# Moving the modulation tiles, the tap tables and the long convolution within a two-layer trunk

## The chip, the cores and the metric

The kernel runs on one core of a Trainium2 chip. The metric is the device time of one execution in microseconds: the median of three runs is 1769.27 us (1768.16 to 1769.97). The core has a matrix engine (PE; PEld is its weight load, which overlaps the products), a vector engine (DVE), a scalar engine (ACT), a second vector-like engine (POOL) and SP, which here issues DMAs. Each takes its instructions in the order in which they stand in its queue, and waits for the others by semaphores.

## The reference

Two layers over 640 tokens (128 context tokens and 512 latent ones) with 1024 channels. Each layer is a mixer and a feed-forward part; each of the two is preceded by a norm, which is scaled and shifted by a modulation that comes from a conditioning vector, and added to the stream through a gate from the same modulation:

```python
mod = silu(cond) @ w_mod[i] + b_mod[i]               # 6 x 1024 values, for 2 kinds of tokens
sh1, sc1, gt1, sh2, sc2, gt2 = split(mod, 6)
hm  = rmsnorm(x, g_mix) * (1 + sc1) + sh1
x   = x + gt1 * mixer(hm)
hf  = rmsnorm(x, g_ffn) * (1 + sc2) + sh2
x   = x + gt2 * conv_ffn(hf)

# mixer of layer 0
proj = hm @ w_in                                     # z, xbc, dt, and the two halves of glu
xbc  = silu(conv5(xbc)); y = ssd_scan(both ways); y_ssd = rmsnorm(y * silu(z))
u    = glu[:1024] * sigmoid(glu[1024:])
u    = silu(layernorm(conv31(u)))                    # the long convolution, per channel
out  = concat(y_ssd, u) @ w_out
```

The mixer of layer 1 is a Fourier transform over tokens and channel groups, with a linear map behind it.

## The kernel before

A channel tile is 128 channels on the partitions and the tokens along the free dimension; 1024 channels are eight tiles. Each product of an fp32 weight tile with the activations is done as three products of split numbers (high by high, high by low, low by high), 48 matmuls of 128x320 per output tile (`mtile`, L233). The weights are split on ACT (a cast) and on POOL (a subtraction). A product collects in a bank pair of PSUM (`acc`); small results use half banks (`misc`).

The order of the work in layer 0 is the order of the code, except where `tc.issue_after(x)` sets the priority of what it holds behind the instruction x. The stages, with their place in the span:

- The start (0 to 74 us). x is loaded, its squares are summed on ACT and DVE (`SumSq`, L330 and L334), and the norm's factor is made (L306). Then for each channel tile k the shift column is made by `mod_tensor` and the scale column by `mod_vector`, the tile is normed and split (`norm_split`), and three products (time steps, first half of the first gated pair) take one tile after another as it comes.
- The gated pairs (74 to 222 us), the loop at L839. Each of eight rounds has two products (14 in all, since the first pair is begun at the start); ACT makes a tanh, DVE the gated product `ut` (L851). Behind each gating come four modulation tiles (`MODSG`), and in the last four rounds some steps of the long convolution (`CONV`).
- The projection of group 0 (222 to 265 us), four products, each followed by a convolution of width 5 on DVE and by one step of the long convolution (`CONVP`).
- The scan (265 to about 500 us): four groups of five chunks. Chunk i+1 is begun (`scan_a`: decay exponents and weights), the fillers of chunk i follow (`project` of the next group, the gates' products, and five steps of the long convolution by `CONVAT`), then `scan_b` (chunk product) and `scan_c` (sum into y, next state). It is written one chunk ahead, so that PE has something between dependent pieces.
- The output products (about 500 to 699 us), first those of y, then those of u, each tile ending in a residual on DVE (L366); between the residuals stand 16 modulation tiles (`YMODS`, `UMODS`).
- The feed-forward part of layer 0 (to 1130 us), with 32 more modulation tiles; the Fourier mixer (to 1297 us); the feed-forward part of layer 1 (to 1769 us). Each works on pairs of channel tiles: two products of about 7 us, a 3x3 convolution on DVE, POOL and PE, and a gating.

Modulation. Of the 96 columns, the first 8 shifts are made on PE (`mod_tensor`, L248: eight matmuls of a weight tile with the 2 conditioning vectors as stationary operand, a copy of the 2 rows, a transpose to columns). All others are made row by row on DVE (`mod_vector`, L272): SP fetches a 128x1024 tile of the transposed weights, and two instructions (L280) multiply it with a conditioning row that has been broadcast to all partitions, and sum along the row; L284 adds the bias. The broadcast rows (`cond_rows`, L266) are fetched from memory by a broadcasting DMA and put through Silu, three times: for the start, for the gated pairs, and for the output products.

The long convolution (`conv_steps`, L590) works in the frequency domain on blocks of 98 tokens. It is a generator of 16 steps; a step has up to three parts on different blocks: `turn` (transposes on PE, copy on ACT), `forth` (transform on PE, two products with the tap tables on DVE), `back` (transform back on PE, addition on DVE, sums on POOL). The tap tables (`tap_tables`, L561) are four small matmuls of the taps with a transform matrix and four copies on ACT, behind DMAs on ACT's queue. They stand ahead of the gated loop (L838).

What the names in the rows mean: `con` the identity and masks, `vec` the small vectors, `crow` the broadcast rows, `mraw` and `rawv` a modulation weight tile, `modc` the finished columns, `mjunk`/`junk` the unused product, `tt` and `tw` the transform matrix and the taps, `dfl` the transform of the long convolution, `cv` its middle, `u` its input and output, `yT` the stream, `yh`/`uh` the split y and u, `wh` the high weights, `xh` the normed activations.

## Time and profile before

| | |
|---|---|
| median of three runs | 1769.27 us |
| profiled execution | 1770.86 us, its span 1769.1 us |
| instructions | 27926 |
| DMA | 194.98 MB, mean 110 GB/s |
| PE's granted clock, mean | 0.969 |

The profile is one execution. Its page gives busy times of each engine over the span; a busy PE is a PE whose matmuls follow one another, at whatever clock was granted. The windows view gives the same for chosen stretches, with the granted clock (1.00 is the upper of its two levels, 2.4 GHz). The timeline gives instructions in order of time with the idle time before them and what ended it. The groups by line add up instructions of one line and form. In every view `128x320 f32` is partitions by elements, and `x12` a count.

### The profile page before, as it was taken

The page shows a single profiled execution, that of the slowest core. Times are in us where ns is not written, and L with a number is a line of the kernel's source. Part 1 is how long each engine was busy: PE and PEld are TensorE (multiplying, and loading weights), DVE is VectorE, ACT ScalarE, POOL GpSimd, SP SyncE. Part 2 cuts the span into 40 slices and gives each one's busy share as a digit, 9 for nine tenths or more (in the row PEclk, how much of TensorE's full clock was granted, in tenths as well). Part 3 has the DMA queues.
Part 4 walks back from the last instruction along what each step waited for, and adds up shares of the span by engine and source line. Part 5 has one row for each costly group of instructions (what it writes and reads, how often), then busy time and mean ns, then how long its engine had stood idle before and what let it go on. Part 6 is the DMA issues. An engine that isn't in the chain of part 4 may idle for free.

```text
span 1769.1 us, 27926 instructions
## 1 busy us (share of the span) xinstructions
PE 1640.6 (93%) x10769; PEld 1574.7 (89%) x10769; DVE 1350.1 (76%) x2392; ACT 700.4 (40%) x1221; POOL 833.0 (47%) x566
## 2 busy tenths in 40 slices
PE   5789999999989878999999999989799999999996
PEld 3589998888968867999999999969799999999996
DVE  6778776677379887899889999873878738817846
ACT  4323154687656134332232133355543313312324
POOL 1134235555667443555455365512536535544544
PEclk8889999999989988999999999989999999999998
DMA  7545431333224543215323522431522222222123
GB/s 284 198 157 192 144 99 60 99 99 112 84 83 155 191 144 120 87 54 152 117 64 115 184 66 62 132 104 42 175 82 69 69 84 79 65 84 72 57 58 113
DMA packets 84677, 194.98 MB, mean 110 GB/s; under 512 B 7843, under 2 KB 35394, under 8 KB 84544
## 3 DMA queue, kind: packets, MB, share of 16 engines
q1 hardware_dynamic: 81216, 189.43, 34.2%
q10 hardware_dynamic: 3328, 3.77, 0.7%
q8 instruction: 85, 1.39, 0.3%
q14 instruction: 48, 0.39, 0.1%
HBM read 189.33 MB, written 3.83 MB: 109 GB/s over the span
## 4 chain that ended last, share of the span: by engine, by line
PE 56%; DVE 10%; ACT 2%; issue 1%; DMA 1%; POOL 1%; DVEq 0%; SPq 0%; ACTq 0%; POOLq 0%
PE acc L233 53%; DVE mm L280 2%; DVE yT L366 2%; DVE ssq L334 2%; DVE hmt L352 1%; PE acc L341 1%; PE misc L233 1%; PE acc L1100 1%; DVE xl L361 1%; ACT sqt L330 1%; DVE yT L1240 1%; DVE modc L284 0%; PE acc L1208 0%; DVE ul L945 0%; DMA mm<-in_condr 0%
## 5 line engine op out<-in xcount | busy, mean ns | idle before, releaser
L225 POOL TENSOR_TENSOR wl<-raw,wh 128x512 fp32r<-128x512 f32 (+5 forms) x324 | 577.8, 1791 | 748.6 <-ACT wh L222 741.4
L233 PE MATMUL acc<-xh,wh 128*128 128x320 f32 (+2 forms) x2064 | 489.6, 315 | 14.9 <-ACT xh L360 6.8
L1038 DVE SCALAR_TENSOR_TENSOR cva<-acc,cw,cva 128x504 f32<-128x504 f32 (+2 forms) x704 | 482.8, 693 | 18.5
L222 ACT CAST wh<-raw 128x512 fp32r<-128x512 f32 (+5 forms) x324 | 244.1, 764 | 628.9 <-PE acc L233 488.9
L233 PE MATMUL acc<-xh,wl 128*128 128x320 f32 (+2 forms) x2064 | 490.6, 314 | 0.0
L233 PE MATMUL acc<-xl,wh 128*128 128x320 f32 (+2 forms) x2064 | 488.8, 314 | 0.4 <-DVE xl L361 0.4
L233 PEld LDWEIGHTS acc<-xh,wh 128*128 128x128 f32 (+1 forms) x2064 | 353.7, 191 | 18.0 <-issue 8.9
L233 PEld LDWEIGHTS acc<-xh,wl 128*128 128x128 f32 (+1 forms) x2064 | 352.7, 190 | 3.6 <-issue 2.5
L233 PEld LDWEIGHTS acc<-xl,wh 128*128 128x128 f32 (+1 forms) x2064 | 352.7, 191 | 3.0 <-DVE xl L361 1.5
L233 PE MATMUL acc<-fh,wl 128*128 128x320 f32 (+2 forms) x832 | 206.1, 310 | 2.8 <-POOL wl L225 2.7
L233 PE MATMUL acc<-fh,wh 128*128 128x320 f32 (+2 forms) x832 | 206.1, 310 | 0.0
L233 PE MATMUL acc<-fl,wh 128*128 128x320 f32 (+2 forms) x832 | 205.7, 310 | 0.0
L366 DVE SCALAR_TENSOR_TENSOR yT<-acc,modc,yT 128x512 f32<-128x512 f32 (+4 forms) x233 | 108.1, 492 | 113.4 <-PE acc L233 111.3
L233 PEld LDWEIGHTS acc<-fh,wl 128*128 128x128 f32 x832 | 143.2, 188 | 4.5 <-POOL wl L225 4.2
L233 PEld LDWEIGHTS acc<-fl,wh 128*128 128x128 f32 x832 | 143.4, 188 | 0.6
L233 PEld LDWEIGHTS acc<-fh,wh 128*128 128x128 f32 x832 | 143.3, 188 | 0.4
L280 DVE SCALAR_TENSOR_TENSOR mm<-mm 128x1024 f32<-128x1024 f32 x84 | 129.3, 1540 | 3.5 <-DMA mm<-in_w_modT 2.7
L1027 DVE SCALAR_TENSOR_TENSOR cva<-acc,cw,cva 128x127 f32<-128x127 f32 x176 | 61.3, 348 | 69.8 <-ACT cva L1023 64.4
L280 DVE SCALAR_TENSOR_TENSOR mjunk<-mraw,crow 128x1024 f32<-128x1024 f32 x64 | 88.5, 1383 | 4.6 <-DMA mraw<-in_w_modT 4.1
L1070 POOL TENSOR_TENSOR fl<-cva,fh 128x640 fp32r<-128x640 f32 x44 | 70.4, 1600 | 35.2 <-ACT fh L1069 35.2
L1066 POOL TENSOR_TENSOR cva<-cva 128x640 f32<-128x640 f32 x44 | 69.8, 1586 | 17.1 <-ACT cva L1065 17.1
L1069 ACT CAST fh<-cva 128x640 fp32r<-128x640 f32 x44 | 32.0, 728 | 100.8 <-POOL cva L1066 100.8
(252 smaller groups left out, 1941.6 us busy)
## 6 DMA issues: line engine op xcount, KB each, us to landing
raw<-in_ffn_w_up SPq DMA_DIRECT2D x88, 512.0 KB, 3.6
mm<-in_w_modT SPq DMA_DIRECT2D x42, 512.0 KB, 3.7
raw<-in_w_in SPq DMA_DIRECT2D x40, 512.0 KB, 3.7
mraw<-in_w_modT SPq DMA_DIRECT2D x32, 512.0 KB, 3.8
e<-acsd SPq DMA_DIRECT2D x40, 256.0 KB, 3.5
raw<-in_ffn_w_down SPq DMA_DIRECT2D x32, 256.0 KB, 2.7
mraw<-in_w_mod SPq DMA_DIRECT2D x14, 512.0 KB, 4.1
raw<-in_ffn_w_down SPq DMA_DIRECT2D x16, 448.0 KB, 3.4
```

Of the source, the lines that this page charges most:

```text
L222: S.copy(wh[:, ks, :], raw[:, ks, :])
L225: G.tensor_tensor(wl[:, ks, :], raw[:, ks, :], wh[:, ks, :].bitcast(F32), op=SUB)
L233: PE.matmul(part(ps, s), lhsT=wt[:, k, :], rhs=tok(at, s), start=(k == 0 and p == 0), stop=(k == n - 1 and p == 2))
L280: V.scalar_tensor_tensor(junk, in0=raw[:, cs_], scalar=1.0, in1=crow[j][:, cs_], op0=MULT, op1=MULT, accum_out=m[:, 2 * o + j:2 * o + j + 1])
L330: S.activation(t, tok(x_ap, s), AF.Square)
L334: V.tensor_tensor(tok(self.a, s), tok(self.a, s), t, op=ADD)
L366: last = V.scalar_tensor_tensor(tok(x[:, m, :], sub), in0=part(ps, s, o, sub), scalar=gt[:, m, j:j + 1], in1=tok(x[:, m, :], sub), op0=MUL ...
L1027: V.scalar_tensor_tensor(a[:, lo:hi], in0=ps[:, BASE + lo + d:BASE + hi + d], scalar=w(1, c), in1=a[:, lo:hi], op0=MULT, op1=ADD)
L1038: last = V.scalar_tensor_tensor(av[:, r0:r1, c0:c1], in0=pv[:, r0 + dr_:r1 + dr_, c0 + dc:c1 + dc], scalar=w(r, c), in1=av[:, r0:r1, c0:c1 ...
L1066: G.tensor_tensor(cv[0], cv[0], cv[1], op=MULT)
L1069: S.copy(h_, cv[0])
L1070: G.tensor_tensor(l_, cv[0], h_.bitcast(F32), op=SUB)
```

## The change

The broadcast rows are made once, at the start: ACT fetches the two conditioning rows as a 2x1024 tile (`crow2`), puts it through Silu, and PE spreads each row to 128 partitions by a product with a selecting matrix (`sel`, made on DVE from the identity); DVE copies them to SBUF, where they stay until the scan ends. The three fetches of broadcast rows go. The tap tables are made at the start too: their four DMAs stand on ACT's queue ahead of the Silu of the rows and the squares, the four matmuls and two copies behind the norm's sums. For the channel tiles 0, 3 and 6 the scale column is made on PE, together with the shift (`SCPE`). The gated rounds have 2, 3, 4, 4, 4, 3, 3, 3 modulation tiles (26 in place of 32). The scan gets 16, one behind the weights of each of its first 16 chunks (`MODSC`). The output products have none. Six go to the first six pairs of the last feed-forward part (`MODS1`). The modulation weight tiles outside the start have two buffers in place of three (`MRAW`). The nine steps of the long convolution that are left after the gated pairs are done within the projection of group 0 (3, 2, 2, 2) in place of one behind each of its four products and one in each of the first five turns of the scan; its buffers are closed before those of the scan are opened, ahead of the fourth product's convolution.

```diff
-SCPE = ()
-MODSG = (4,) * 8
+SCPE = (0, 3, 6)
+MODSG = (2, 3, 4, 4, 4, 3, 3, 3)
+MODSC = (1,) * 16 + (0,) * 4
-CONVP = 1
-CONVAT = {0: 1, 1: 1, 2: 1, 3: 1, 4: 1}
+CONVP = (3, 2, 2, 2)
-YMODS = (0,)*5+(2,2,1,1,0,0,0,0)
-UMODS = (2,2,2,2,2,0,0,0)
-MRAW = 3
+MRAW = 2
-MODS1 = ({}, ((0,) * 8,) * 3)
+MODS1 = ({j: 1 for j in range(6)}, ((0,) * 8,) * 3)
...
+    con = one.tile([P, 3 * P], F32, name="con")
+    S.dma_start(con, A["consts"])
     vec = one.tile([P, NV], F32, name="vec")
     S.dma_start(vec, A["vec"])
-    con = one.tile([P, 3 * P], F32, name="con")
-    S.dma_start(con, A["consts"])
...
+        crow2 = sp.tile([P, D], F32, name="crow2")[0:2, :]
+        S.dma_start(crow2, A["condr"])
+        tw = [temp(f"tw{h}")[0:CK, 0:HC] for h in range(2)]
+        tt = sp.tile([P, 2 * P], F32, name="tt")[0:CK, :]
+        S.dma_start(tt, A["dftk"])
+        for h in range(2):
+            S.dma_start(tw[h], A["conf_w"][:, HC * h:HC * h + HC])
+        S.dma_start(dfl, A["dftl"])
         for k in range(0, KD, 2):
             nc.sync.dma_start(xin[:, k:k + 2, 0:T], A["xT"][:, k:k + 2, :])
-        crow = cond_rows(sp)
+        S.activation(crow2, crow2, AF.Silu)
+        sel = sm.tile([P, 384], F32, tag="sqt", name="sel", bufs=3)[0:2, 0:2 * P]
+        prow = []
+        for j in range(2):
+            V.tensor_copy(sel[:, P * j:P * j + P], ident[0:2, j:j + 1].broadcast_to([2, P]))
+            prow.append(acc())
+            for h in range(2):
+                PE.matmul(prow[j][:, HC * h:HC * h + HC], lhsT=sel[:, P * j:P * j + P], rhs=crow2[:, HC * h:HC * h + HC], start=True, stop=True)
         rsqrt_table(eps)
...
+        for j in range(2):
+            V.tensor_copy(crow[j], prow[j])
...
-        for t in crow:
-            S.activation(t, t, AF.Silu)
+        for i in range(2):
+            ps = acc()
+            for h in range(2):
+                PE.matmul(ps[:, HC * h:HC * h + HC], lhsT=tt[:, P * i:P * i + P], rhs=tw[h], start=True, stop=True)
+            S.copy(tap[i], ps)
...
-            V.scalar_tensor_tensor(e1[:, h, :], in0=cm[:, 0, :], scalar=dt[:, c, i:i + 1], in1=e1[:, h, :], op0=MULT, op1=ADD)
+            last = V.scalar_tensor_tensor(e1[:, h, :], in0=cm[:, 0, :], scalar=dt[:, c, i:i + 1], in1=e1[:, h, :], op0=MULT, op1=ADD)
+        with tc.issue_after(last.ins):
+            mods_n(MODSC[5 * g + c])
...
-    mcrow = cond_rows(md)
-    for t in mcrow:
-        S.activation(t, t, AF.Silu)
-    mjunk = md.tile([P, D], F32, name="mjunk")
...
-    tap_tables()
...
-    md_.__exit__(None, None, None)
+    first = project(0, R[0])
+    for f, n in zip(first[:3], CONVP):
+        f()
+        convolve(n)
+    convolve(CONVP[3])
+    assert next(conv, 0) == 0
+    cw_.__exit__(None, None, None)
+    cp_.__exit__(None, None, None)
     mz = tc.tile_pool(name="mz", bufs=1)
     mzp = mz.__enter__()
-    for f in project(0, R[0]):
-        f()
-        convolve(CONVP)
+    first[3]()
...
-    for i, n in CONVAT.items():
-        fillers[i].append(lambda n=n: convolve(n))
...
     def after_w(m, ps):
-        with tc.issue_after(residual(x, m, ps, gt, ALL).ins):
-            mods_y(UMODS[m])
+        residual(x, m, ps, gt, ALL)
```

How this stands in the queues of the engines, at three places. First ACT's queue from its beginning. A number behind a name tells tiles of one name apart; `DMAHW0` to `DMAHW7` are eight landing counters that the DMAs use in turn. Before:

```order
L172 DMA cond_75<-in_cond 128x16
L174 DMA vec_77<-in_vec 128x280
L176 DMA con_79<-in_consts 128x384
L300 ACT_TABLE_LOAD
L300 ACTIVATE tab_112<-eps_84 128x1 [waits DVE_49]
L244 ACT_TABLE_LOAD
L244 ACTIVATE sc__86<-cond_75 128x16 [waits DMAHW0_49]
L330 ACTIVATE ssq_115<-xin_94 128x320 [waits DMAHW1_49]
```

And with the change:

```order
L172 DMA con_77<-in_consts 128x384
L174 DMA vec_79<-in_vec 128x280
L438 DMA crow2_117<-in_condr 2x1024
...
L441 DMA tt_121<-in_dftk 31x256
L443 DMA tw0_119<-in_conf_w 31x512
L443 DMA tw1_120<-in_conf_w 31x512 [waits DMAHW2_49]
L444 DMA dfl_111<-in_dftl 128x324 [waits DMAHW3_49]
L447 ACTIVATE crow2_117<-crow2_117 2x1024 [waits DMAHW4_49]
L290 ACT_TABLE_LOAD
L290 ACTIVATE tab_140<-eps_83 128x1 [waits DVE_49]
L320 ACTIVATE ssq_142<-xin_93 128x320 [waits DMAHW1_49]
```

The first square (L330, now L320) has moved behind the issue of the tap tables' DMAs, two of which wait for the landing of con and vec, and behind the Silu of the short rows.

Second DVE's queue in the scan, in one chunk of group 0 (`w` the weights, `e` the exponents, `hn` the next state, `cm` the chunk's masked product, `y` and `yT` sums). Before:

```order
L787 SCALAR_TENSOR_TENSOR w<-cm,dt,w 128x128 x4
L803 TENSOR_TENSOR e<-misc,eacs 128x512
L770 TENSOR_TENSOR e<-e 128x512
L728 TENSOR_TENSOR hn<-misc,hd 128x256
L822 TENSOR_TENSOR yT<-misc,yT 128x128 x2
L777 TENSOR_TENSOR cm<-misc,con 128x256
L813 TENSOR_TENSOR y<-misc,y 128x256
```

And with the change:

```order
L802 SCALAR_TENSOR_TENSOR w<-cm,dt,w 128x128 x3
L270 SCALAR_TENSOR_TENSOR mjunk,mm<-mraw,crow_106 128x1024
L839 TENSOR_TENSOR yT<-misc,yT 128x128
L270 SCALAR_TENSOR_TENSOR mjunk,mm<-mraw,crow_107 128x1024
L839 TENSOR_TENSOR yT<-misc,yT 128x128
L274 TENSOR_SCALAR modc_87<-mm,vec 128x2
L785 TENSOR_TENSOR e<-e 128x512
L743 TENSOR_TENSOR hn<-misc,hd 128x256
L830 TENSOR_TENSOR y<-misc,y 128x256
```

Two products of a modulation tile and its bias now stand between the chunk's weights and the exponents, the next state and the sum of y that follow.

Third DVE's queue in the output products of u (L366 and L356 are the residuals). Before:

```order
L366 SCALAR_TENSOR_TENSOR yT<-acc,modc_88,yT 128x512
L280 SCALAR_TENSOR_TENSOR mm_5230,mm<-mm_5230 128x1024
L366 SCALAR_TENSOR_TENSOR yT<-acc,modc_88,yT 128x128
L284 TENSOR_SCALAR modc_89<-mm,vec 128x2
L280 SCALAR_TENSOR_TENSOR mm_5230,mm<-mm_5230 128x1024
L366 SCALAR_TENSOR_TENSOR yT<-acc,modc_88,yT 128x512
```

And with the change:

```order
L356 SCALAR_TENSOR_TENSOR yT<-acc,modc_87,yT 128x128
L356 SCALAR_TENSOR_TENSOR yT<-acc,modc_87,yT 128x512
L356 SCALAR_TENSOR_TENSOR yT<-acc,modc_87,yT 128x128
L356 SCALAR_TENSOR_TENSOR yT<-acc,modc_87,yT 128x512
```

Between the residuals nothing of the modulation is left.

## Rows read from the trace of the kernel before

**Rows 1.** The profile's page: busy time of each engine, share of the span, instructions.

```profile
PE 1640.6 (93%) x10769; PEld 1574.7 (89%) x10769; DVE 1350.1 (76%) x2392; ACT 700.4 (40%) x1221; POOL 833.0 (47%) x566
```

**Rows 2.** Windows: stretch, us, PE, PEld, DVE, ACT, POOL busy, PEclk, DMA share, GB/s.

```profile
1350.00:1375.00 25.00, 25.00 (x172) 25.00 (x171) 22.96 (x39) 9.03 (x12) 15.88 (x8) 1.00 0.19 52
```

**Rows 3.** Windows of the projection, the scan's first three groups, the output products.

```profile
222.00:265.00 43.00, 42.50 (x289) 39.24 (x287) 32.80 (x51) 26.38 (x52) 16.57 (x17) 1.00 0.31 95
265.00:332.00 67.00, 61.66 (x398) 56.31 (x398) 43.04 (x82) 32.89 (x70) 38.37 (x48) 0.97 0.25 76
332.00:385.20 53.20, 50.14 (x340) 48.02 (x340) 37.79 (x79) 40.94 (x88) 28.61 (x33) 1.00 0.35 99
385.20:435.80 50.60, 45.98 (x301) 42.34 (x300) 38.75 (x82) 41.30 (x93) 28.88 (x32) 1.00 0.36 104
550.00:650.00 100.00, 82.15 (x540) 79.65 (x538) 91.26 (x141) 35.99 (x58) 61.87 (x38) 0.94 0.53 173
```

**Rows 4.** Timeline: start us, us, engine, line, operation [idle before <- releaser], the start.

```profile
5.27 0.81 ACT L330 ACTIVATE ssq<-xin 128x320 f32<-128x320 f32 x2
...
7.93 0.19 DVE L180 TENSOR_SCALAR vec<-vec 128x56 f32<-128x56 f32 x1 [6.10 <-DMA vec<-in_vec]
...
12.95 1.99 ACT L439 ACTIVATE crow<-crow 128x1024 f32<-128x1024 f32 x2
...
14.96 1.28 ACT L306 ACT_TABLE_LOAD   x1
...
30.97 0.74 PE L233 MATMUL acc<-xh,wh 128*32 128x320 f32 x2 [4.23 <-ACT xh L360]
```

**Rows 5.** DMA issues of the first 30 us: KB each, median us to landing.

```profile
con<-in_consts ACTq DMA_DIRECT2D x1, 192.0 KB, 8.3
```

**Rows 6.** Groups by line, PE, 31 to 73.9: busy us, mean ns, idle before.

```profile
L254 PE MATMUL misc<-mraw,sc__86 128*2 128x128 f32 x80 | 9.9, 272 | 0.0
```

**Rows 7.** Timeline of PE around its longest waits before the scan.

```profile
83.77 3.75 PE L569 MATMUL misc<-tw,tt 31*128 31x512 f32 x4 [9.88 <-DMA tt<-in_dftk]
...
90.96 1.98 PE L569 MATMUL misc<-tw,tt 31*128 31x512 f32 x4
...
122.65 0.88 PE L233 MATMUL acc<-xh,wh 128*128 128x320 f32 x2 [5.66 <-DVE u L851]
```

**Rows 8.** Windows right behind the first and the last of these waits.

```profile
87.45:92.87 5.42, 5.42 (x18) 3.84 (x17) 2.38 (x5) 2.68 (x4) 0.00 (x0) 0.68 0.02 6
122.65:128.65 6.00, 6.00 (x23) 6.00 (x24) 6.00 (x17) 0.00 (x0) 0.00 (x0) 0.51 0.38 117
```

**Rows 9.** Groups by line, DVE, gated pairs from 87 to 222 us.

```profile
L280 DVE SCALAR_TENSOR_TENSOR mjunk<-mraw,crow 128x1024 f32<-128x1024 f32 x53 | 74.8, 1411 | 0.9 <-DMA mraw<-in_w_modT 0.6
...
L284 DVE TENSOR_SCALAR modc<-mm,vec 128x2 f32<-128x2 f32 x26 | 11.7, 452 | 0.3
...
L280 DVE DVE_READ_ACCUMULATOR mjunk<-mraw,crow 128x1 f32 x52 | 4.2, 81 | 0.0
```

**Rows 10.** Line L280 in the same stretch: shortest, median, longest in ns.

```profile
L280 DVE SCALAR_TENSOR_TENSOR mjunk<-mraw,crow x53: 1208/1223/2311, 87.1 to 221.9; 128x1024 f32<-128x1024 f32 x53
```

**Rows 11.** Windows of tile dfl (PE, PEld), long convolution in the scan.

```profile
265.00:340.00 75.00, 13.60 (x88) 10.87 (x88) 0.98 0.25 78
```

**Rows 12.** The same of tile u (PE, PEld, DVE, ACT, POOL).

```profile
265.00:340.00 75.00, 1.80 (x12) 1.42 (x12) 2.67 (x5) 0.00 (x0) 5.79 (x6) 0.98 0.25 78
```

**Rows 13.** The same of tile cv (PE, PEld, DVE).

```profile
265.00:340.00 75.00, 9.89 (x80) 9.63 (x80) 5.48 (x8) 0.98 0.25 78
```

**Rows 14.** Waits of the whole span: total us, times, longest.

```profile
PE acc L233 <- DVE yT L366: 8.0, 6, 2.5
```

**Rows 15.** Timeline of PE in the output products.

```profile
546.27 0.38 PE L233 MATMUL acc<-yh,wh 128*128 128x256 f32 x1 [1.87 <-ACT yh L896]
...
588.39 0.55 PE L233 MATMUL misc<-yh,wh 128*128 128x256 f32 x1 [6.43 <-DVE yT L366]
...
595.09 0.53 PE L233 MATMUL acc<-uh,wh 128*128 128x320 f32 x2 [1.67 <-issue]
```

More of the change, by code (lines that the diff above doesn't have):

```diff
@@ L434, in _body @@
                 ss.add(xin[:, k, :], k, s)
+        for j in range(2):
+            V.tensor_copy(crow[j], prow[j])
+        V.tensor_scalar_mul(vec[:, 0:NGAIN], vec[:, 0:NGAIN], -0.5 / D)
         bc0 = ss.bc
@@ L471, in _body @@
         pd, pg0, pa0 = (ps for ps, _ in first)
[L473 to L474 removed]
+    cw_ = tc.tile_pool(name="cw", bufs=1)
+    cw = cw_.__enter__()
     def t640(name):
@@ L597, in forth @@
             PE.matmul(ps, lhsT=dfl[:, 0:P], rhs=xt.pop((h, b)), start=True, stop=True)
-            vv[h, b] = [mxp.tile([P, HC], F32, tag=f"cv{i}", name=f"cv{i}", bufs=2) for i in range(2)]
+            vv[h, b] = [cw.tile([P, HC], F32, tag=f"cv{i}", name=f"cv{i}", bufs=2) for i in range(2)]
             for i in range(2):
@@ L972, in _body @@
                 y_segment(CHUNKED[c == 4])
-    assert next(conv, 0) == 0
     mz.__exit__(None, None, None)
+    md_.__exit__(None, None, None)
     mx.__exit__(None, None, None)
@@ L978, in _body @@
     yp = yp_.__enter__()
[L979 to L986 removed]
     def after_w(m, ps):
[L990 to L991 removed]
+        residual(x, m, ps, gt, ALL)
     while ytodo:
         n = ny - len(ytodo)
[L995 to L996 removed]
+        y_product()
         if n == LNY:
```

92 lines of the change are left out of this document (36 added, 56 removed).

## The prediction

> **What bounds the kernel now.** I read the page first, then the busy times by stage, the timeline of PE around its longest waits, the groups of instructions by line, and the waits. On the page the reader is to see that PE is busy for 93% of the span [rows 1], so only what keeps PE waiting, or what it does besides the products, can give time back. By stage this is not spread evenly. The two feed-forward parts hold PE at 25 of 25 us [rows 2]; nothing is to be had there. PE waits in three other places: around the end of the first norm and the tap tables (0 to 129 us), in the scan (265 to 436 us, where PE is busy 61.7 of 67.0, 50.1 of 53.2 and 46.0 of 50.6 us [rows 3]), and in the output products after it (550 to 650 us, where DVE is busy 91.3 of 100 and PE 82.2 [rows 3]). The change touches all three. All sums are made against the profiled execution, 1770.86 us (span 1769.1 and 1.8 around it); it lies 1.6 above the median of the runs, and I take that off at the end.
>
> **The start, up to the first gated product: +2 us.** Two things are moved here, the tap tables and the broadcast of the conditioning rows, and three scale tiles go from DVE to PE. Before, ACT started its squares at 5.27 us [rows 4]. In the new order ACT first issues four more DMAs, and two of them wait for the landing of con and vec, because DMAs share eight landing counters in turn. The con DMA, issued third before, took 8.3 us to land [rows 5], until about 10.0 us of the span; vec was there at 7.93 [rows 4]. With their order swapped I take 10.0 for the later one. Behind it stand the Silu of the short rows (free length 1024, half of the 1.99 us of two such [rows 4]) and a table load of 1.28 [rows 4]: squares at about 12.3 us, 7 later. A table load and two tap copies of 1024 (1.0 each by the same row) stand among them, another 3. The first main product would be released about 10 us later than 30.97 [rows 4], but before it waited for DVE, whose two row-wise tiles stood between the norm and hmt; I take 8. PE then also has 3 more tiles of the small product, 1.98 us each (9.9 us for five tiles [rows 6]): 6 us, of which 4.9 tiles of all now stand ahead of the first main product, beside the late norm. From there to the end of the stretch (73.9 us, where the wait of 9.88 begins [rows 7], 42.9 us after the first product) DVE has five row-wise tiles less, 15 us at their shortest price of 3.0 (below). PE's own need is 144 products at 0.145 (172 in 25 us [rows 2]), 6.1 tiles of 1.98, and about 3 of transposes: 36 instead of 42.9. So +8 - 6 = +2. From both sides: -6 if vec and con land as early as 8 us and the rest hides, +10 if the main stretch stays as long as it is.
>
> **The stretch of gated products: -23.8 us.** Behind the last product of the start PE stands for 9.88 us until the tap tables' data lands, and then spends 3.75 on two of the four tap products [rows 7]: the next product comes at 87.45, 13.55 us late. The following 5.42 us run at a granted clock of 0.68 [rows 8], between the two levels of 1.2 and 2.4 GHz, after PE had stood; a third of it, 1.7, is lost. The other two tap products take 1.98 [rows 7]. All of that goes, if the tables are made while PE has nothing to do at the start. Then there is one wait of 5.66 for DVE's gating [rows 7], followed by 6.00 us at 0.51 of the clock [rows 8], 2.9 lost: DVE came to that gating late because four row-wise tiles stood ahead of it, held by rows that were still landing and being put through Silu, and the time-step arithmetic as well. With two and three tiles in the first two rounds instead of four and four it is in time. Sum 25.8. I give back 2: the buffers for the row-wise tiles are cut from three to two, so the rows of a tile can be asked for only when the tile before the last is done. The bounds are -28, and -15 if DVE stays late.
>
> What is late next is DVE in each round. A row-wise tile costs two L280 of 1.41, two reads of the accumulator (0.08) and one L284 of 0.45 [rows 9, 10]: 3.43 us, and at the least 2 x 1.21 + 0.16 + 0.45 = 3.0. Four are 13.7 of a round of 14 (96 products), so DVE nearly fills it; with three of them in rounds 5 to 7 it is looser than before.
>
> **The scan: +23.6 us.** Five steps of the long convolution leave the scan, 13.60 + 1.80 = 15.4 us of PE and 2.67 + 5.48 = 8.2 of DVE [rows 11 to 13]. They go to the four products before the scan, where PE is busy 42.5 of 43.0 us [rows 3]; so the 15.4 are added there in full. The scan's first three groups took 67.0 + 53.2 + 50.6 = 170.8 us. Without the steps PE needs 157.8 - 15.4 = 142.4 there. DVE had 43.0 + 37.8 + 38.8 = 119.6; minus 8.2, plus 15 of the 16 tiles at 3.43 (51.5): 162.9 us. So DVE becomes the bound of these groups. Nowhere in this trace is it busier than in the output products, 91% [rows 3], where it is the bound; 162.9 / 0.91 = 179, that is 8.2 more than now. The sum is 15.4 + 8.2. The fourth group has one tile and much idle DVE; I charge nothing. The bounds: DVE without any idle time gives 162.9, a sum of +7.5; every tile on the path in full gives 170.8 - 15.4 + 51.5, a sum of +51.5. The nearest row is that of a bounding DVE, so I stay with 0.91.
>
> A tile is queued on DVE right behind a chunk's last weight. What stands behind it there is the off-diagonal product of the chunk before, the sum into y and the next state; PE's next state, transposes and chunk product wait for these, and PE already waited for such a state now and then. So part of each tile must be expected to reach PE.
>
> **The output products: -23 us.** All 16 tiles leave this part. PE waited eight times: 8.0 us in six waits for the residual on DVE, 6.43 for a bank that a residual had not freed, 1.67 behind the casts of an ACT that stood for rows being landed, and 1.87 for yh, held up by the Silu on the rows just fetched [rows 14, 15]: 18.0 together. The granted clock over these 100 us is 0.94 [rows 3]; 6 us lost, some of it while PE stood anyway, so 5. DVE is left with 91 - 16 x 3.43, some 36 us of 77, and is no bound any more. POOL is the next busiest with 61.9 [rows 3], and part of that is waiting for DVE. The bounds: -10 if POOL's splitting of weights holds PE, -30 if the norm's end gains too.
>
> **The second feed-forward: +1 us.** Six tiles move to its first six pairs of channels. DVE is busy 22.96 of 25 us there [rows 2], so a pair of 14 us has 12.8 of DVE; with a tile 16.4. It falls behind by 2.4 a pair, 14 in all. Four product banks allow PE to be about three products of 7 us ahead, less one conv of 6.4, so about 14.5. A stall of 1 us or none; 8 if the lag at the start of the part counts in full.
>
> **Edits at no cost.** Rows kept in SBUF instead of fetched again save six DMAs of 512 KB and as many Silus, counted above where PE waited for them. Memsets and the scaling of the gains move on DVE to where it has time.
>
> Sum: 2 - 23.8 + 23.6 - 23 + 1 = -20.2, that is 1750.7 for an execution like the profiled one, 1749 for the median.
>
> **Rivals.**
> First, the scan hides the tiles: PE's filler products (20 of them in the scan) are long enough for DVE to work meanwhile, DVE runs without a gap, and the scan's term is 7.5: 1733. For it speaks that DVE idles 51 of 170.8 us now; against it that its queue is in order and PE's is too.
>
> Second, the other side: the scan is a chain, not a sum. Place: behind each of 15 chunks' weights; price 3.43 each, 51.5 in all, with 15.4 saved in the scan and added before it; time 2 - 23.8 + 51.5 - 23 + 1 = +7.7, so 1777. It decides from the point at which more than 44 of the 51.5 reach PE. For it speaks that ACT, DVE and PE wait for one another within one chunk; against it that most chunks have a 7 us product beside them.
>
> Third, the change doesn't do what it says at the start: the tap wait is moved, not removed. The tables' DMAs queue behind x and the first weights, ACT holds the squares for the tap copies, and the 13.6 come back: 1763. PE did stand 9.88 us for the tables' data where they are fetched now; but 7 more than now are already in my first term.
>
> Fourth, a fight of DVE and POOL. In the trace L280 goes from 1.21 to 2.31 us [rows 9, 10], and POOL is busy 54 to 57% in the scan [rows 3]. If each L280 there waited out the rest of a POOL instruction that often, it would cost 1.21 + 0.55 x 1.1 = 1.81 and a tile 4.15; 15 x 0.72 / 0.91 = 12 more: 1761. The Trainium skill, in the page SBUF — State Buffer, section Who interferes with whom, speaks for this: a DVE instruction with both inputs in SBUF and a GpSimd instruction that reads SBUF shut each other out for the whole instruction. The spread of L280 agrees with it; its mean of 1.41 says that it happens one time in five or six.
>
> **Chances.** The forecast 54%, from 1737 to 1761; the scan hides 16%; slower by the chain 10%; the start 10%; the fight 10%. Of the first, a little ends within 0.2% (3.5 us, about what a measurement of this kernel can tell from no change), and of the third and fourth rival a quarter. That makes faster 83%, same 7%, slower 10%. The range leaves out the far end of the second rival and what lies below the first: 1722 to 1772.
>
> **What would show it.** Right: no wait for tap data after the start's last product; PE's first main product some 8 us later than now; the four products before the scan longer by 15; DVE over 90% busy through the first three groups of the scan, and PE waiting there for DVE's states and sums; no modulation tile between the residuals, and PE without waits for them. Wrong: a PE in the scan that waits no more than now (then the first rival), or a scan over 200 us for the three groups (then the second); or ACT standing at a tap copy while the squares are due.

## The result, and the profile after

The changed kernel takes 1795.89 us (median of 4 runs, 1793.79 to 1797.99) against 1769.62 of the kernel before; the ratio is 1.0148 with the interval 1.013 to 1.0165. It is slower by 26 us, outside the range of the prediction and on the other side.

The table below is made from the traces: "first product" is the start of the first three-pass matmul, a gating ends with the second DVE instruction `u<-sg,acc` of a round, a chunk with its fourth `w<-cm,dt,w`, and "convolution" is the end of the first 3x3 instruction of the first feed-forward part. Times in us from the span's start; the last column is how much longer the stretch became, beside what was predicted.

| end of the stretch | before | after | stretch longer by | predicted |
|---|---|---|---|---|
| first product | 31.0 | 48.6 | +17.6 | +8 |
| first gating | 74.8 | 87.1 | -5.3 (start in all +12.3) | start +2 |
| third gating | 122.5 | 122.0 | -12.8 | |
| eighth gating | 217.2 | 215.6 | -1.1 (gated in all -13.9) | -23.8 |
| first chunk | 269.2 | 293.2 | +25.5 | +15.4 |
| sixteenth chunk | 439.5 | 487.3 | +23.8 | +8.2 |
| twentieth chunk | 497.8 | 541.8 | -3.8 | 0 |
| convolution | 704.0 | 725.1 | -22.8 | -23 |
| end | 1769.1 | 1795.9 | +5.6 | +1 |

The page's first section, to set beside [rows 1], shows the same share of PE, so the share says nothing of where the 27 us are:

```profile
PE 1661.3 (93%) x10828; PEld 1586.7 (88%) x10828; DVE 1351.3 (75%) x2384; ACT 701.4 (39%) x1217; POOL 853.7 (48%) x566
```

By stage it is plain. First the kernel before, from the eighth gating to the first chunk and from there to the sixteenth; columns as in [rows 2]:

```profile
217.00:269.20 52.20, 51.70 (x350) 47.99 (x349) 40.59 (x64) 28.26 (x58) 23.78 (x25) 1.00 0.31 96
...
269.20:439.50 170.30, 157.29 (x1036) 146.09 (x1035) 118.83 (x244) 116.62 (x255) 93.61 (x107) 0.99 0.31 91
```

Then the same stretches of the changed kernel, with the fourth group of the scan and 100 us of the output products:

```profile
215.60:293.20 77.60, 72.92 (x466) 65.74 (x465) 43.93 (x75) 26.91 (x54) 31.95 (x41) 0.93 0.23 72
...
293.20:487.30 194.10, 158.07 (x951) 147.67 (x950) 159.68 (x307) 123.60 (x263) 111.64 (x95) 0.89 0.40 121
487.30:541.80 54.50, 51.12 (x349) 50.18 (x347) 28.03 (x57) 39.47 (x82) 37.42 (x32) 1.00 0.28 88
...
578.00:678.00 100.00, 92.44 (x619) 90.61 (x619) 53.31 (x91) 44.01 (x75) 55.38 (x43) 0.98 0.36 116
```

In the scan DVE has the 159.7 us that the prediction gave it (162.9), but it is busy for 82% of the stretch and not for 91%: it isn't the bound. PE stands, that is, it is idle, for 36.0 us (194.10 - 158.07; before 13.0), and it is busy as long as before though 15.4 us of work have left, at a granted clock of 0.89 in place of 0.99. In the output products no wait of PE for a residual is left; DVE went from 91.3 to 53.3 us of 100 (the prediction had 36 of 77) and the clock from 0.94 [rows 3] to 0.98.

The start, on ACT (start us, us, operation, idle time before and what ended it), beside [rows 4]:

```profile
12.45 0.81 ACT L320 ACTIVATE ssq<-xin 128x320 f32<-128x320 f32 x2
13.16 0.81 ACT L320 ACTIVATE sqt<-xin 128x320 f32<-128x320 f32 x2
...
16.09 1.28 ACT L544 ACT_TABLE_LOAD   x1
23.49 0.23 ACT L544 ACTIVATE nega<-rows 128x32 f32<-128x32 f32 x1 [6.11 <-DMA rows<-in_rows]
23.62 1.17 ACT L320 ACTIVATE sqt<-xin 128x320 f32<-128x320 f32 x3
24.70 0.99 ACT L471 COPY tap<-acc 128x1024 f32<-128x1024 f32 x1
25.60 1.19 ACT L320 ACTIVATE sqt<-xin 128x320 f32<-128x320 f32 x3
27.25 1.01 ACT L471 COPY tap<-acc 128x1024 f32<-128x1024 f32 x1 [0.47 <-PE acc L470]
```

The squares begin at 12.45, where the prediction had them (12.3). But among them now stands an Exp of the time steps' bias rows (L544), which waits for a DMA, and the tap copies. The last square ends at 29.2 in place of 13.0. On PE meanwhile:

```profile
10.98 7.19 PE L454 MATMUL acc<-crow,sel 2*128 2x512 f32 x8 [10.98 <-ACT crow L447]
17.97 1.91 PE L470 MATMUL acc<-tw,tt 31*128 31x512 f32 x2
21.73 5.49 PE L470 MATMUL acc<-tw,tt 31*128 31x512 f32 x6 [1.85 <-DMA tw<-in_conf_w]
27.41 1.43 PE L331 MATMUL misc<-ssq,ones 128*128 128x320 f32 x2 [0.20 <-DVE ssq L324]
```

The tap products stand ahead of the norm's sums (L331) and hold them until 27.2 as well. Two holds end within two microseconds of each other; the experiments tell them apart.

In the gated pairs the wait for the tables is gone, but not the one for the third gating, which was 5.66 [rows 7]; behind it the clock is still low (the second fence, windows, to set beside [rows 8]):

```profile
122.20 0.87 PE L229 MATMUL acc<-xh,wh 128*128 128x320 f32 x2 [7.78 <-DVE u L856]
```

```profile
122.00:128.00 6.00, 5.80 (x28) 5.83 (x29) 5.96 (x16) 0.00 (x0) 0.00 (x0) 0.68 0.24 89
```

Before the scan PE now waits for steps of the long convolution and for what follows the last of them; the window of 229 to 240 us shows the clock around and behind the first two waits:

```profile
230.47 0.43 PE L622 MATMUL misc<-dfl,cv 128*128 128x98 f32 x2 [1.31 <-DVE cv L615]
231.77 3.31 PE L622 MATMUL misc<-dfl,cv 128*128 128x98 f32 x14 [0.69 <-DVE cv L615]
281.75 0.44 PE L716 MATMUL misc<-con,cvx 128*128 128x128 f32 x2 [2.23 <-ACT xb L718]
```

```profile
229.00:240.00 11.00, 8.99 (x41) 7.61 (x41) 7.69 (x12) 3.62 (x5) 0.00 (x0) 0.69 0.26 92
```

In the scan this is what one tile does, on DVE (L687 is a convolution of width 5 whose end frees a product bank, L270 and L274 the tile):

```profile
388.07 0.87 DVE L687 SCALAR_TENSOR_TENSOR cvb<-acc,vec,cvb 128x640 f32<-128x640 f32 x1
388.86 1.12 DVE L802 SCALAR_TENSOR_TENSOR w<-cm,dt,w 128x128 f32<-128x128 f32 x4
389.91 1.21 DVE L270 SCALAR_TENSOR_TENSOR mjunk<-mraw,crow 128x1024 f32<-128x1024 f32 x1
...
391.05 0.87 DVE L687 SCALAR_TENSOR_TENSOR cvb<-acc,vec,cvb 128x641 f32<-128x641 f32 x1
391.85 1.48 DVE L270 SCALAR_TENSOR_TENSOR mjunk<-mraw,crow 128x1024 f32<-128x1024 f32 x1
...
393.26 0.88 DVE L687 SCALAR_TENSOR_TENSOR cvb<-acc,vec,cvb 128x641 f32<-128x641 f32 x1
394.05 0.42 DVE L274 TENSOR_SCALAR modc<-mm,vec 128x2 f32<-128x2 f32 x1
394.39 0.87 DVE L687 SCALAR_TENSOR_TENSOR cvb<-acc,vec,cvb 128x640 f32<-128x640 f32 x1
```

and on PE, which has no bank for its next product until that convolution ends, and is then busy for 6 us at 0.72 of the clock (the second fence, windows):

```profile
395.41 0.87 PE L229 MATMUL acc<-xh,wh 128*128 128x320 f32 x2 [5.95 <-DVE cvb L687]
```

```profile
389.50:395.50 6.00, 0.09 (x1) 0.12 (x1) 6.00 (x12) 1.21 (x4) 5.44 (x3) 0.71 0.32 98
395.50:401.50 6.00, 6.00 (x34) 5.88 (x35) 1.44 (x6) 5.96 (x10) 1.36 (x3) 0.72 0.50 179
```

DVE gets to its next work with time to spare: at 401.27 it has idled for 4.6 us. It is not out of time, it is late at one point.

### The profile page after: what moved, and what is told of

It reads as the page before. It is cut to its first block, busy times and chain, and to the rows that moved or that the text cites. A ratio compares the mean times of both kernels' runs of the same rounds, so it can differ in the third digit from the quotient of the medians.

```text
span 1795.9 us, 28008 instructions
## 1 busy us (share of the span) xinstructions
PE 1661.3 (93%) x10828; PEld 1586.7 (88%) x10828; DVE 1351.3 (75%) x2384; ACT 701.4 (39%) x1217; POOL 853.7 (48%) x566
## 4 chain that ended last, share of the span: by engine, by line
PE 64%; DVE 24%; DMA 4%; ACT 3%; POOL 3%; issue 2%; SPq 0%; DVEq 0%; ACTq 0%; POOLq 0%
PE acc L229 56%; DVE cva L1035 4%; DVE mjunk L270 4%; DVE ssq L324 2%; DVE yT L356 2%; DVE hmt L342 2%; DMA mraw<-in_w_modT 1%; DVE mm L270 1%; DVE w L802 1%; PE misc L622 1%; DMA e<-acsd 1%; PE acc L331 1%; PE misc L250 1%; POOL wl L221 1%; DMA tw<-in_conf_w 1%
## 5 line engine op out<-in xcount | busy, mean ns | idle before, releaser
L1035 DVE SCALAR_TENSOR_TENSOR cva<-acc,cw,cva 128x441 f32<-128x441 f32 (+2 forms) x704 | 477.6, 691 | 16.2
L356 DVE SCALAR_TENSOR_TENSOR yT<-acc,modc,yT 128x512 f32<-128x512 f32 (+4 forms) x233 | 107.2, 493 | 126.3 <-PE acc L229 125.5
L229 PEld LDWEIGHTS acc<-fh,wl 128*128 128x128 f32 x832 | 143.2, 188 | 4.7 <-POOL wl L221 4.4
L270 DVE SCALAR_TENSOR_TENSOR mjunk<-mraw,crow 128x1024 f32<-128x1024 f32 x84 | 125.9, 1499 | 7.4 <-DMA mraw<-in_w_modT 7.0
L270 DVE SCALAR_TENSOR_TENSOR mm<-mm 128x1024 f32<-128x1024 f32 x64 | 104.1, 1626 | 0.8
L1020 ACT ACTIVATE cva<-acc,cw 128x640 f32<-128x640 f32 x88 | 69.4, 789 | 0.0
```

What stands on the lines that cost most here:

```text
L229: PE.matmul(part(ps, s), lhsT=wt[:, k, :], rhs=tok(at, s), start=(k == 0 and p == 0), stop=(k == n - 1 and p == 2))
L270: V.scalar_tensor_tensor(junk, in0=raw[:, cs_], scalar=1.0, in1=crow[j][:, cs_], op0=MULT, op1=MULT, accum_out=m[:, 2 * o + j:2 * o + j + 1])
L356: last = V.scalar_tensor_tensor(tok(x[:, m, :], sub), in0=part(ps, s, o, sub), scalar=gt[:, m, j:j + 1], in1=tok(x[:, m, :], sub), op0=MUL ...
L1020: S.mul(a, ps[:, BASE:BASE + T], w(1, 1))
L1035: last = V.scalar_tensor_tensor(av[:, r0:r1, c0:c1], in0=pv[:, r0 + dr_:r1 + dr_, c0 + dc:c1 + dc], scalar=w(r, c), in1=av[:, r0:r1, c0:c1 ...
```

## The experiments

Stretches below are those of the table. The first four kernels ask of the scan and the start.

**The scan's tiles back between the residuals.** The diff is that of the change reversed for `MODSC`, `YMODS`, `UMODS` and the rows of the output products:

```diff
-MODSC = (1,) * 16 + (0,) * 4
+MODSC = (0,) * 20
+YMODS = (0,)*5+(2,2,1,1,0,0,0,0)
+UMODS = (2,2,2,2,2,0,0,0)
```

Expected: 

> The changed kernel with one part undone: the 16 modulation tiles of the scan stand between the residuals of the output products again, with broadcast rows fetched for them as before the change; the long convolution stays ahead of the scan. From the end of the first chunk's weights to that of the sixteenth it was 170.3 us before and 194.1 with the change. Theory C (the tiles make the scan late): this stretch falls to about 155, which is 170.3 less the 15.4 of PE work that has left; the output products get their 26 us back; 1796 - 39 + 26 = 1783. Rival D (it is the long convolution that the scan misses, as work for PE while it waits): the stretch stays at 170 or more, and the time is 1798 or more.

Measured: 1777.94 us, ratio 1.0047 (1.0032 to 1.0062). From the first chunk to the sixteenth:

```profile
292.90:449.00 156.10, 143.19 (x934) 134.79 (x934) 112.79 (x233) 122.04 (x262) 87.13 (x95) 0.99 0.36 104
```

156 against the 155 of theory C; rival D falls. PE stands 12.9 us, the clock is 0.99. So 15 tiles cost 38.0 us there, 2.54 each: (36.0 - 12.9) / 15 = 1.54 of standing, and 1.0 of PE being busy for longer, at a clock of 0.89 in place of 0.99. Among the output products the 16 cost 204.5 - 183.3 = 21.2, 1.3 each. It also prices the move of the long convolution without the tiles: from the eighth gating to the sixteenth chunk this kernel takes 233.4 us, before it was 222.3, which is 11.1 more. But its fourth group takes 52.9 in place of 58.3, so at the end of the scan only 5.7 of them are left. PE's waits in the scan, total, times and longest, first with the tiles and then without:

```profile
PE acc L229 <- DVE cvb L687: 14.6, 3, 5.9
PE misc L814 <- POOL e L810: 8.6, 4, 6.5
PE misc L790 <- DVE hn L743: 5.3, 4, 2.4
PE acc L229 <- DVE cvx L687: 3.8, 1, 3.8
```

```profile
PE misc L737 <- ACT hn L740: 3.4, 2, 2.5
PE misc L792 <- DVE hn L745: 2.6, 4, 1.1
PE misc L718 <- ACT cvb L691: 1.5, 1, 1.5
```

The second wait with the tiles is for POOL, and POOL is slower beside them: the same 95 instructions took 111.6 us in place of 87.1. Its product `e<-e,w` is released by the same last weight behind which the tile stands on DVE. It took 2.1 to 2.3 us in 13 of the 15 chunks with a tile, and 1.3 in all 15 of this kernel. The groups by line, with the tiles and then without:

```profile
L810 POOL TENSOR_TENSOR e<-e,w 128x512 f32<-128x512 f32 x15 | 31.2, 2077 | 14.7 <-DVE w L802 14.7
```

```profile
L812 POOL TENSOR_TENSOR e<-e,w 128x512 f32<-128x512 f32 x15 | 19.3, 1287 | 25.9 <-DVE w L804 25.9
```

How much of the 2.54 us of a tile comes by way of POOL was not tried apart.

**The tiles away from the convolutions.**

```diff
-MODSC = (1,) * 16 + (0,) * 4
+MODSC = (1, 0, 1, 0, 1) * 3 + (2, 2, 1, 1, 1)
```

Expected: 

> The changed kernel with the 16 tiles put elsewhere in the scan: none behind the weights of the second and fourth chunk of a group, where the two convolutions of width 5 follow on DVE; 9 in the first three groups and 7 in the fourth, in place of 15 and 1. The stretch of the first fifteen chunks took 194.1 us with 15 tiles. Theory L (a tile costs where it stands ahead of, or among, the convolutions that must free a product bank, 14.6 + 3.8 us of waits and the lower clock behind them): the waits of products for these convolutions go, the stretch falls to 165 or less, 1770 or less in all. Rival M (every tile delays the chain of the scan by the same, (194.1 - 155) / 15 = 2.6 us): 9 tiles leave 155 + 23 = 178, and the fourth group gets 16 more: 1796.

Measured: 1789.66 us, ratio 1.0107 (1.009 to 1.0125). The first fifteen chunks, and the four behind:

```profile
291.00:470.60 179.60, 155.25 (x951) 146.39 (x951) 141.79 (x276) 120.02 (x261) 100.88 (x95) 0.92 0.39 116
470.60:534.50 63.90, 55.90 (x354) 54.88 (x353) 47.44 (x84) 40.72 (x83) 43.07 (x32) 0.92 0.37 116
```

PE's waits for convolutions fell from 18.4 to 4.4 us, as theory L has it, but the other waits stayed (17.4 and now 19.8, for six tiles fewer): 179.6 is the 178 of rival M. 9 tiles cost (179.6 - 156.1) / 9 = 2.6 each, 15 cost 2.54. In the fourth group it is (63.9 - 52.9) / 6 = 1.8, less than M's price, and the whole time lies between L's and M's. A price that does not rise with the number, while DVE's busy share goes from 72% without tiles to 79 and 82%, is that of a chain, not of an engine that is full.

**The bias rows out of the squares' way.**

```diff
-    rows = mxp.tile([P, 64], F32, name="rows")
+    rows = cw.tile([P, 64], F32, name="rows")
```

Expected: 

> The changed kernel with one edit: the tile of the time steps' bias rows lies in the pool that is opened only after the start, so that its DMA and the Exp on ACT can't be put among the squares of the first norm. Theory A (ACT is held): in the changed kernel ACT stands 6.1 us for the rows to land and loads a table (1.28) between two squares; without these the first main product comes at about 41 us in place of 48.6, and the kernel takes some 7 us less, 1789. Rival B (PE is held): PE has the four tap products queued ahead of the norm's sums, and these wait for their data until 21.7 and end at 27.2; then the sums can begin no earlier than 27.2 either way, and the gain is 2 us or less, 1794.

Measured: 1791.79 us, ratio 1.0128 (1.0107 to 1.0148); the first product at 47.5 (1.1 earlier), the first gating 1.9 earlier. At the start rival B is right: without the Exp, ACT stood 6.22 us for the first tap copy instead. The median fell by 4 us, more than B said, but the interval overlaps that of the changed kernel, and 2.3 us of the difference of the two profiles lie in the output products, which the edit doesn't touch.

**And the tap products behind the start's last product.** The four products and two copies move below the loop over the channel tiles; `tw` gets buffers of its own.

Expected: 

> As the kernel with the bias rows moved, and the tap products and their copies stand behind the last product of the start; their data is still fetched at the beginning. Theory A (ACT is held): little more than with the rows alone, the first main product at 40 to 41 us, and 2 us of tap products later on PE: 1789 to 1791. Rival B (PE is held by the tap products): only now the start shortens, the first main product comes at 39 or earlier, 9 us before that of the changed kernel, against 2 with the rows alone: 1787.

Measured: 1792.01 us, ratio 1.0129 (1.0109 to 1.0149). The first product came at 43.3, 5.3 earlier than with the change, where the rows alone had given 1.1, the first gating at 80.3, 6.8 earlier: the tap products had hidden what the rows' move was worth. But the stretch to the third gating took 39.0 in place of 34.9, since PE now makes the tap products there; the end of the gated pairs is that of the kernel with the rows moved.

**And the selecting matrix with a buffer of its own.**

```diff
-        sel = sm.tile([P, 384], F32, tag="sqt", name="sel", bufs=3)[0:2, 0:2 * P]
+        sel = mxp.tile([P, TG], F32, tag="t640", name="sel", bufs=5)[0:2, 0:2 * P]
```

Expected: 

> As the kernel with the bias rows moved and the tap products behind the start, and the selecting matrix no longer shares the buffers of the squares (there a square waited 2.14 us until PE had used it). Nothing then stands between the squares on ACT any more. Theory A (what lengthened the start were things put among the squares, one behind the other, so that each that goes shows the next; all gone, the squares take the 7.8 us that they took before): they end at 12.3 + 7.8 = 20 to 21 us in place of 29.2, and the first main product comes at 39 to 40, 8 or 9 later than before the change. Rival B (x lands later than before, so the squares wait for it): they end at 23 or later, the product comes at 42 or later.

Measured: 1787.57 us, ratio 1.0097 (1.0066 to 1.0129). On ACT nothing stands among the squares:

```profile
12.19 0.81 ACT L320 ACTIVATE ssq<-xin 128x320 f32<-128x320 f32 x2
12.90 5.50 ACT L320 ACTIVATE sqt<-xin 128x320 f32<-128x320 f32 x14
```

They end at 18.4, earlier than the 20 to 21 of theory A, the first product comes at 38.3 and the first gating 2.3 later than before the change. That is the start as it was predicted (+8, and +2 in all). Three holds made the other 10 us.

**Fewer tiles ahead of the third gating, and the convolution's steps in another split.**

```diff
-MODSG = (2, 3, 4, 4, 4, 3, 3, 3)
+MODSG = (3, 1, 4, 4, 4, 4, 3, 3)
...
-CONVP = (3, 2, 2, 2)
+CONVP = (2, 2, 2, 3)
```

Expected: 

> The changed kernel with two edits in stages that don't meet: the gated rounds have 3, 1, 4, 4, 4, 4, 3, 3 tiles in place of 2, 3, 4, 4, 4, 3, 3, 3, and the steps of the long convolution stand as 2, 2, 2, 3 among the four products before the scan in place of 3, 2, 2, 2. In the changed kernel PE waits 7.8 us for the third gating. Theory A (DVE is late there because three tiles and some 25 instructions of time-step arithmetic stand between two gatings): with two tiles less, 6.9 us, the wait falls to about 1, and the end of the last gating comes 6 to 9 us earlier (the lower clock behind the wait goes too). Rival B (the arithmetic alone, or the wait for its inputs, makes it late): the wait stays above 5. For the convolution, theory C (three steps behind the first product are too dense: PE waits 2.0 us for DVE's products with the taps at 229 to 232 us and then runs at 0.50 to 0.69 of the clock for 8 us): the stretch from the last gating to the first chunk's weights falls from 77.6 to 72 or 73; rival D (the cost is a sum over steps, wherever they stand): it stays within 1.5 of 77.6. All together 1780 to 1784 by A and C, 1795 by B and D.

Measured: 1790.24 us, ratio 1.0103 (1.008 to 1.0125). The wait for the third gating fell from 7.8 to 4.5, the last gating came 3.1 earlier: between the two theories. The stretch to the first chunk took 78.6, so rival D holds: waits of 1.17 and 0.69 stayed where they were, and that behind the last step grew from 2.23 to 3.10.

**The time-step arithmetic later.**

```diff
-DTAT = 1
+DTAT = 4
...
-DTAT2 = 4
+DTAT2 = 5
```

Expected: 

> The changed kernel with the time-step arithmetic behind the fifth gating in place of the second, and its second part behind the sixth; tiles and convolution as in the changed kernel. Theory A (it is this arithmetic, queued on DVE between the second and third gating, that makes PE wait 7.8 us for the third): the wait falls below 1, the third gating ends at 114 to 115 in place of 122, and the last gating ends 5 to 8 us earlier, since the later rounds have steps of the long convolution for PE meanwhile: 1788 to 1790. Rival B (DVE is as late with the tiles alone, or as late where the arithmetic stands now): a wait of 5 or more for the third or the sixth gating, the last gating no more than 2 us earlier, 1794.

Measured: 1799.01 us, ratio 1.0162 (1.013 to 1.0193). PE's waits on the long convolution and on the gating, from 84 to 240 us:

```profile
PE misc L622 <- DVE cv L615: 15.0, 4, 12.5
PE acc L229 <- DVE u L856: 1.1, 1, 1.1
```

The wait for the third gating is gone and that gating ended at 115.6: the cause is the arithmetic, with the tiles ahead of it. But a single wait of 12.5 for the long convolution's products, which now stand behind the arithmetic, came in its place, up to 178 us, and the last gating was 7.8 later. That is nearest to the second half of rival B (as late where the arithmetic stands now), though for another piece of work than B named.

**The last feed-forward part without tiles.**

```diff
-MODSG = (2, 3, 4, 4, 4, 3, 3, 3)
+MODSG = (4,) * 8
...
-MODS1 = ({j: 1 for j in range(6)}, ((0,) * 8,) * 3)
+MODS1 = ({}, ((0,) * 8,) * 3)
```

Expected: 

> The changed kernel with the six tiles of the last feed-forward part moved into the gated pairs, which then have 4 in each of their eight rounds. Theory A (these six tiles cost what the last feed-forward part got longer, 5.5 us): that part takes 394.9 us again as before the change. Theory B for the gated pairs (DVE fills a round with four tiles): the six cost up to 3.4 each there, 20 us; rival (DVE has room in the first and the last rounds): 3 or less in all. In sum 1793 or less by the rival, up to 1811 by B.

Measured: 1790.25 us, ratio 1.0092 (1.0065 to 1.0119). That part, from its first to its last 3x3 convolution, took 394.9 us as before, against 400.3 with the six tiles; the gated pairs got 1.9 longer. In the changed kernel PE had waited there four times for DVE:

```profile
PE acc L229 <- DVE cva L1035: 4.5, 4, 2.3
```

These waits lie at 1385 to 1431 us, 62 to 108 us into the part. The tiles were dearer there than the 3.43 us of the prediction: by the groups on DVE from 1323 to 1450 us, (21.2 + 8.3 + 0.9) / 6 = 5.1 each, where the 0.9 are the accumulator's reads:

```profile
L270 DVE SCALAR_TENSOR_TENSOR mm<-mm 128x1024 f32<-128x1024 f32 x12 | 21.2, 1765 | 0.0
L274 DVE TENSOR_SCALAR modc<-mm,vec 128x2 f32<-128x2 f32 x6 | 8.3, 1383 | 0.0
```

**The tap tables alone, in the kernel before.** The four DMAs go to POOL's queue at the start, products and copies behind the start's last product, nothing else of the code changes.

Expected: 

> The kernel before with one part of the change alone, made so that ACT's and PE's queues at the start stay as they were: the tap tables' data is fetched by DMAs on POOL's queue at the beginning, and their four products and two copies stand behind the last product of the start. Nothing else is changed. Theory A (the wait of 9.88 us for the tables' data is worth taking away, and the round that follows gives part of it back, since DVE's work between the second and third gating, 19.4 us, stays the bound there): the second gating ends at 92 in place of 103.1, the third at 113 in place of 122.5, and the kernel takes 1760 (9 less). Rival B (DVE's row-wise tiles of the first round, which start when their rows land, hold the second gating): it stays later than 98, and the kernel takes 1766 or more.

Measured: 1766.86 us, ratio 0.997 (0.9955 to 0.9984). Rival B: the second gating ended at 101.9 and PE waited 9.8 for the third, because DVE began its first tile at 87.0, when its rows and weights were there:

```profile
84.31 0.39 DVE L522 TENSOR_TENSOR dtmp<-misc,rows 128x32 f32<-128x32 f32 x3 [16.53 <-DMA rows<-in_rows]
...
87.00 1.23 DVE L280 SCALAR_TENSOR_TENSOR mjunk<-mraw,crow 128x1024 f32<-128x1024 f32 x1 [1.31 <-DMA mraw<-in_w_modT]
...
88.94 1.23 DVE L280 SCALAR_TENSOR_TENSOR mjunk<-mraw,crow 128x1024 f32<-128x1024 f32 x1 [0.71 <-ACT crow L829]
```

In the kernel before, the first tile had begun at 78.34:

```profile
78.34 1.23 DVE L280 SCALAR_TENSOR_TENSOR mjunk<-mraw,crow 128x1024 f32<-128x1024 f32 x1 [3.51 <-DMA mraw<-in_w_modT]
```

So it is the edit that made the rows late. SP issued their fetch at 77.8, when the last tap product had ended, in place of 69.6; ACT issued that of the time steps' bias rows at 78.1, behind the tap copies, in place of 69.7; and DVE stood 16.53 us for these, with the first gating behind it, which ended at 85.5 in place of 74.8. The hold came back in another place, and this run doesn't show what the end of the tables' wait alone is worth. **With the arithmetic later as well** (`DTAT = 4`, `DTAT2 = 5`):

Expected: 

> The kernel before with the tap tables made behind the start's last product, their data fetched on POOL's queue, as tried, and with the time-step arithmetic behind the fifth gating (its second part behind the sixth). With the tap tables alone PE waited 9.8 us for the third gating. Theory A (the arithmetic makes it wait): the wait falls to 2 or less, and the kernel takes 1757 to 1760. Rival B (DVE is late there because its first tiles had to wait for broadcast rows that are fetched only when the start's memory is free): the wait stays above 5, and the kernel takes 1764 or more.

Measured: 1781.17 us, ratio 1.0065 (1.004 to 1.0091): the third wait was still 7.0 (B, in its mechanism), and one of 13.3 came behind it at 168 us.

**Two versions to beat both.** The tap tables as just tried and, for one, the rounds' tiles as 2, 3, 4, 4, 4, 5, 5, 5:

Expected: 

> The kernel before with the tap tables made behind the start's last product (their data fetched on POOL's queue), as tried, and with the gated rounds' modulation tiles as 2, 3, 4, 4, 4, 5, 5, 5 in place of eight times 4. With the tap tables alone PE waited 9.8 us for the third gating, after eight tiles and the time-step arithmetic. Theory A (three tiles less ahead of it take about that much DVE work away, at 2.7 to 3.4 us each): the wait falls to 1 to 3 us, the lower clock behind it shortens, and the time comes to 1757 to 1760, if the three tiles fit into the last rounds, where DVE was busy 33.7 of 43 us. Rival B (the last rounds have no room for them): what is won at the third gating comes back as a later end of the last gating, and the time stays at 1765 to 1768.

Measured: 1765.39 us, ratio 0.9976 (0.9961 to 0.999), not to be told from the tables alone (0.997). The wait fell from 9.8 to 6.9 only, and the last rounds had room (the last gating 3.7 earlier than with the tables alone); neither theory had its number. For the other, the changed kernel with all but the long convolution's place mended:

Expected: 

> The changed kernel with what the runs so far showed to be dear mended and only the long convolution's place left as in the change: squares of the start free of other work (bias rows, selecting matrix, tap products moved as tried), the scan's 16 tiles among the residuals of the output products again, but with the broadcast rows that are kept in SBUF, the six tiles of the last feed-forward part in the gated rounds (2, 3, 4, 4, 4, 5, 5, 5). Theory A (the parts add up): 1786.1 of the mended start, less 20.3 for the scan's tiles (194.1 to 156.0 us in the scan, 1.6 in its fourth group, 21.2 back in the output products, 1.8 elsewhere), less 5.5 and plus about 2 for the six tiles: 1762 to 1764, and the move of the long convolution (11 us by the runs) is what it has left over the time that the rest would give. Rival B (the parts hide one another, as the holds of the start did): 1770 or more.

Measured: 1768.36 us, ratio 0.9988 (0.9977 to 0.9998); the span of its profile is 1765.5. Theory A, which was worked out from spans, had 1762 to 1764, so the parts add up to within 3 us; rival B's 1770 is further off. Its stretch from the eighth gating to the sixteenth chunk took 231.5 against 222.3, and to the twentieth chunk 284.4 against 280.6.

## Why the prediction was wrong

Between the predicted -20.2 and the measured +26.8 us (of the spans) lie 47. The scan's term has 22 of them (45.6 measured, 23.6 predicted), the start 10.3, the gated pairs 9.9, the last feed-forward part 4.6.

The scan: the step that failed is "DVE becomes the bound of these groups", 162.9 / 0.91. DVE's busy time was right to 3 us, the rule to divide it was not. A tile in a queue delays whatever stands behind it, and in the scan that frees PE's banks or feeds the next state. The prediction named this itself (part of each tile must be expected to reach PE), but its sum went by DVE's busy share and not by what waits behind a tile. The second rival had the mechanism (10%) and set 3.43 a tile; it was 2.54, and 1.0 of these is longer busy time of PE at the lower clock, which no term held. The first rival (the scan hides them) is out by the waits above. The fourth, the clash with POOL, is small on DVE: the mean of L270 in the scan is 1.5 us by its group of instructions against 1.41 [rows 9]. It falls on POOL, which needs 24.5 us more (111.6 - 87.1) and on which PE waits 8.6 us in place of 0.9; the rival priced DVE alone.

The four products ahead of the scan: "15.4 are added there in full" took PE's time of the moved steps and no wait. The stretch grew by 25.5; its window shows 4.7 of standing (77.60 - 72.92, before 0.5) and a clock of 0.93, about 5 us of 72.9. That the steps are too dense behind the first product was tried, and did not bear out; which order would hide them stays open. The fourth group gave back 3.8 (5.4 without the tiles), where the prediction charged nothing.

The gated pairs: the tables' part was right in size (to the second gating 14.9 us won, predicted 17.2). "With two and three tiles in the first two rounds instead of four and four it is in time" failed: the arithmetic of the time steps, named in the sentence before it, stood there unchanged, and the 8.6 us did not come. The other cause named there, rows that were still landing, was a misreading: in the kernel before, the first tile began at 78.34, and DVE had stood 12.36 us for PE when the second gating came; the four tiles between the second and the third gating ran without a wait for rows.

The start: "8 later" counted what the diff had written ahead of the squares, not what the scheduler could now put among them. The bias rows' tile had lain in memory that was free only after the start; its pool is opened earlier now, so DMA and Exp could move up among the squares. The piece of that queue shown ahead of the prediction ends at the first square, so neither stands in it. The second hold were the tap products and their copies, as the third rival said (the tap wait is moved, not removed); with the rows gone they cost 4.2 us (47.5 to 43.3) and not its 13.6. The third was the selecting matrix, which took a buffer of the squares, 5.0 us (43.3 to 38.3). No term held the first and the third.

The last feed-forward part: "a stall of 1 us or none" was 5.5. The term that was mis-sized is the tile, 5.1 us there in place of 3.43: DVE falls behind by about 4 us a pair (12.8 + 5.1 - 14) and not by 2.4. With that the same sum gives a stall of some 9 us, more than came. The first wait came 62 us into the part, so the lag at its beginning (8 at the worst) was not shown to be the cause.

The output products were right, -22.8 for -23, and by the mechanism named: with the tiles put back they took 21.2 more.

Two slips in the sums change nothing: the waits of PE in the output products are nine, not eight, and a tile with L280 at 1.81 is 4.23 with both reads of the accumulator, which makes the fourth rival 13 us and not 12.

## What to carry to other kernels

Price a piece of work that is put into another engine's queue by what stands behind it there, one place at a time; whether the engine has idle time left over the stage decides nothing when the stage is a chain. Where a pool is opened earlier, read the whole queue for instructions that its memory had held back. Where one wait is taken away, look for the second that ended just before it: of the three holds at the start the first to go gave 1.1 us, all three 10.3. And ask what the moved work now stands ahead of: the tap copies behind the start held the fetch of rows that a gating needed.

## What was not expected of the hardware

Short waits of PE were followed by a lower granted clock: behind 2.0 us of standing up to 231.8 us came 4 us at 0.50 and 4 at 0.69 (windows of 232 to 236 and 236 to 240 us), and in the scan 1.54 us of standing per tile came with 1.0 us more of busy time. PE's busy time there grew to 158.1 us, for 951 recorded matmuls, from 143.2 for 934.

The clash of DVE and POOL showed on POOL: beside a tile its `e<-e,w` of 128x512 took 2.1 to 2.3 us in place of 1.3 us, while the mean of DVE's 128x1024 product went only from 1.41 to 1.5 us.
